# A hybrid recurrent block on one core: weights stored by loaded block, the input stored transposed, and a redone S5 and first feed-forward block

## The chip, the cores and the metric

The kernel runs on one core of a Trainium2 chip. A core has five engines with instruction streams of their own: TensorE (PE; its weight loads are shown apart as PEld), VectorE (DVE), ScalarE (ACT), GpSimd (POOL) and SyncE (SP), which here only issues DMAs. Each stream is executed in its own order; semaphores tie the streams together. Data lie in HBM, in SBUF (128 partitions) and, for the results of TensorE, in PSUM. The metric is the device time of one execution in microseconds (us), the median of the runs.

## The reference, cut to what matters

One trunk layer over 256 latent and 256 context tokens of width 2048, batch 1, all in float32:

```python
mod_x, mod_c = split(silu(c) @ w_mod + b_mod, 6), split(silu(c_ctx) @ w_mod + b_mod, 6)
hx = modulate(rmsnorm(x,   norm_mix), mod_x[0], mod_x[1])      # h * (1 + scale) + shift
hc = modulate(rmsnorm(ctx, norm_mix), mod_c[0], mod_c[1])
cols = h @ w_in                       # 15 column groups, 15376 wide
# four token mixers over cols, forward and backward: HGRN2, retention, S5, mLSTM
# S5: x_t = lam * x_{t-1} + B u_t (complex diagonal, 32 groups of 64 states), y = Re(C x)
y  = sum_j sigmoid(gate_j) * (branch_j @ w_branch[j])
x1 = x + mod_x[2] * (y @ w_out)
h2 = modulate(rmsnorm(x1, norm_mlp), mod_x[3], mod_x[4])
x2 = x1 + mod_x[5] * (square(relu(h2 @ w_ff1)) @ w_ff2)        # 2048 -> 8192 -> 2048
out = rmsnorm(x2, final_norm)
```

All weights together are some 400 MB, read once.

## The kernel before

**Products.** A weight block is loaded as a unit of 256 rows x 512 columns (512 KB, tile `raw`, `unit`, L80) from the row-major weight, so each partition receives two rows of 2 KB. ScalarE rounds it to a high part `wh` (L59), VectorE subtracts to get the low part `wl` (L35), and TensorE adds three products (high x high, low x high, high x low, all at L62) into PSUM. `run_t` gives results with channels on partitions, `run_n` with tokens on partitions; `run_pair` (first feed-forward weight) uses two products, with high and low part of the input side by side. `raw` has four buffers, `wh` and `wl` four each.

**Order.** The program is written as Python generators that are stepped in turn; a scheduler in the framework then places the instructions of each engine by priority. Weight loads and splits run at high priority. What is final is one fixed instruction order per engine; an instruction whose operand is late holds back all behind it on its engine.

**Opening** (`build`, `norm_in`, `mods_in`, `modulate_in`). Parameter rows are loaded by eleven small DMAs and turned into columns by two transposes on TensorE. The tokens are loaded with tokens on partitions, ScalarE sums the squares, VectorE scales each token row. The first two modulations (33.5 MB of `w_mod`) are made in eight rounds of 256 columns: eight loads (`mraw` or `raw`, 128 x 4 x 256, rows of 1 KB), 64 small products into `macc`, a copy, four transposes and three VectorE operations give the columns `modc`. Then two 128-channel pieces of the input are transposed (four transposes each, `m<-ident,x`, L65), modulated by ScalarE from PSUM (`full`), and split into `hh` and `hl`. Beside the rounds run the projections to the S5 input (`gu`, accumulators `g`) and to the mLSTM query (`gq`, accumulators `q`), half a unit at a step. The S5 parameters are loaded after the first round (`s5_load`, L387); `s5_rows` and `s5_cols` work out the powers of the S5 eigenvalues in some 150 small VectorE operations on 32 x 128 tiles, which TensorE then transposes.

**S5.** Time is cut into 128 steps of four tokens. For each of four groups J and two directions d, `s5_weights` builds B and C weights and the table of rotations `E` (complex, 4 x 128) on VectorE, `s5_states` multiplies the inputs `V` by the rotations (`W`), runs a real scan along time (`tensor_tensor_scan`, L609, eight of 128 steps), and rotates back (`X`). TensorE work on the projections to the mLSTM key, value and gate stands between.

**From the output projection to the feed-forward part** (`tail`). For each 512 columns of `w_out` the result is added to the residual `x2`, squares are summed, and the columns are transposed and scaled (`x2T`). When all are there, the reciprocal norm is worked out and broadcast by TensorE (`m<-ident,rs`), VectorE multiplies all of `x2T` by it, and ScalarE and VectorE make the high and low part `h`. Only then does `run_pair` start on `w_ff1`. At the end of a `run_pair` block each of four accumulators is read, added, squared behind the ReLU and split (`ev1`).

## Time and profile before

| | us |
|---|---|
| median of 3 runs | 2060.59 (2057.99 to 2060.61) |
| profiled execution, whole time | 2053.74 |
| profiled execution, span from first to last instruction | 2052.0 |
| TensorE busy | 1964.0 (96%) |
| TensorE weight loads busy | 1611.0 |
| VectorE busy | 1468.0 (72%) |
| ScalarE busy | 1054.5 (51%) |
| DMA | 410.85 MB, mean 200 GB/s |

A busy share is a mean over stages that differ: TensorE is all but full from 700 us on, and has its gaps before that, at the change to the feed-forward part, and at the end. A matmul's own duration (about 390 ns for 512 columns) overlaps with the next; how fast they follow each other is read from the chain or a window, where 156 of them take about 35.5 us.

### The profile page before, as it was taken

What the parts mean: (1) busy time and instruction counts of PE and PEld (TensorE: products, weight loads), DVE (VectorE), ACT (ScalarE), POOL (GpSimd) and SP (SyncE); (2) the same over time, 40 slices, a digit from 0 to 9 for tenths busy, and PEclk for the clock granted to TensorE, in tenths of its full rate; (3) what the DMA queues carried; (4) which work ended last, traced back from release to release, by engine and by line L of the source; (5) the groups of instructions that cost most, each with busy time, mean ns of one, the idle gap of its engine ahead of it and who ended that gap; (6) DMA issues with size and microseconds to landing.
All of it is one profiled execution on the core that took longest, in us unless ns stands there. A gap on an engine that the chain in (4) does not pass through costs nothing.

```text
span 2052.0 us, 30756 instructions
## 1 busy us (share of the span) xinstructions
PE 1964.0 (96%) x11129; PEld 1611.0 (79%) x11129; DVE 1468.0 (72%) x2924; ACT 1054.5 (51%) x1957; POOL 28.2 (1%) x42
## 2 busy tenths in 40 slices
PE   5899999999999999999999999899999999999998
PEld 2566777777988888878888887788888888888886
DVE  2678887587469776888888885677667766666665
ACT  4245445644486555454545455555555445544554
POOL 0000010000000000000000000000000000000000
PEclk9999999999999999999999999999999999999999
DMA  9993212322442456889888876466777676556654
GB/s 325 280 302 102 73 52 83 108 73 68 133 124 83 160 189 201 311 278 315 286 306 296 309 244 236 157 218 224 244 232 225 227 247 187 189 193 192 189 194 154
DMA packets 237652, 410.85 MB, mean 200 GB/s; under 512 B 23064, under 2 KB 58168, under 8 KB 236732
## 3 DMA queue, kind: packets, MB, share of 16 engines
q1 hardware_dynamic: 234864, 402.74, 59.6%
q10 hardware_dynamic: 2636, 6.16, 0.9%
q8 instruction: 87, 1.43, 0.3%
q14 instruction: 65, 0.53, 0.1%
HBM read 406.75 MB, written 2.10 MB: 199 GB/s over the span
## 4 chain that ended last, share of the span: by engine, by line
PE 69%; issue 19%; DVE 5%; DMA 3%; ACT 3%; SPq 1%; POOL 0%; POOLq 0%; DVEq 0%; ACTq 0%
PE g L62 55%; PE m L62 10%; DMA raw<-in_w_mod 2%; DVE wl L35 1%; PE m L65 1%; PE macc L62 1%; ACT wh L59 1%; PE q L62 1%; PE t L62 1%; DVE modacc L53 1%; DVE s5V L609 0%; SPq L387 0%; DMA x<-in_ctx 0%; DVE s5t L35 0%; ACT full L56 0%
## 5 line engine op out<-in xcount | busy, mean ns | idle before, releaser
L59 ACT CAST wh<-raw 128x512 fp32r<-128x512 f32 x1116 | 687.5, 622 | 719.5 <-PE g L62 316.6
L35 DVE TENSOR_TENSOR wl<-raw,wh 128x512 fp32r<-128x512 f32 x1116 | 757.1, 689 | 369.3 <-ACT wh L59 356.2
L62 PE MATMUL g<-wh,hh 128*128 128x512 f32 x832 | 327.6, 394 | 2.4 <-ACT kd L59 2.4
L62 PE MATMUL g<-wl,hh 128*128 128x512 f32 x832 | 327.3, 393 | 0.0
L62 PE MATMUL g<-wh,hl 128*128 128x512 f32 x832 | 326.5, 392 | 0.0
L62 PE MATMUL g<-wh,aT 128*128 128x512 f32 x992 | 307.1, 390 | 0.0
L53 DVE SCALAR_TENSOR_TENSOR modacc<-raw,cx,modacc 128x512 f32<-128x512 f32 x240 | 179.5, 748 | 55.4 <-DMA raw<-in_w_mod 54.4
L62 PEld LDWEIGHTS g<-wh,aT 128*128 128x128 f32 x992 | 186.2, 188 | 39.3 <-ACT wh L59 0.5
L62 PE MATMUL m<-h,wh 128*128 128x512 f32 x512 | 191.9, 398 | 4.5 <-DVE relu L35 4.5
L62 PE MATMUL g<-h,wh 128*128 128x512 f32 x512 | 191.9, 399 | 2.8 <-DVE h L53 2.8
L62 PE MATMUL g<-wl,aT 128*128 128x512 f32 x496 | 193.0, 389 | 0.0
L62 PEld LDWEIGHTS g<-wh,hh 128*128 128x128 f32 x832 | 156.5, 188 | 37.5 <-ACT wh L59 3.4
L62 PEld LDWEIGHTS g<-wh,hl 128*128 128x128 f32 x832 | 156.6, 188 | 32.9 <-issue 1.0
L62 PEld LDWEIGHTS g<-wl,hh 128*128 128x128 f32 x832 | 156.7, 188 | 32.1 <-DVE wl L35 1.1
L62 PE MATMUL g<-hh,wh 128*128 128x512 f32 (+1 forms) x448 | 159.1, 356 | 5.4 <-ACT wh L59 5.4
L62 PE MATMUL g<-hh,wl 128*128 128x512 f32 (+1 forms) x448 | 158.0, 354 | 0.6 <-DVE wl L35 0.5
L62 PE MATMUL g<-hl,wh 128*128 128x512 f32 (+1 forms) x448 | 157.8, 352 | 0.0
L62 PE MATMUL g<-h,wl 128*128 128x256 f32 x512 | 143.6, 281 | 0.0
L62 PE MATMUL m<-h,wl 128*128 128x256 f32 x512 | 143.4, 280 | 0.0
L62 PEld LDWEIGHTS m<-h,wh 128*128 128x128 f32 x512 | 96.6, 189 | 28.7 <-PE m L62 3.4
L62 PEld LDWEIGHTS g<-h,wh 128*128 128x128 f32 x512 | 96.6, 189 | 26.3 <-DVE h L53 3.1
L62 PEld LDWEIGHTS g<-wl,aT 128*128 128x128 f32 x496 | 93.1, 188 | 19.7 <-issue 0.2
(502 smaller groups left out, 2539.0 us busy)
## 6 DMA issues: line engine op xcount, KB each, us to landing
raw<-in_w_ff SPq DMA_DIRECT2D x256, 512.0 KB, 4.0
raw<-in_w_in SPq DMA_DIRECT2D x242, 512.0 KB, 3.8
raw<-in_w_mod SPq DMA_DIRECT2D x160, 512.0 KB, 4.9
mraw<-in_w_mod SPq DMA_DIRECT2D x32, 512.0 KB, 7.4
raw<-in_w_branch SPq DMA_DIRECT2D x32, 512.0 KB, 3.8
raw<-in_w_out SPq DMA_DIRECT2D x32, 512.0 KB, 4.0
x<-in_ctx SPq DMA_DIRECT2D x2, 1024.0 KB
x<-in_x SPq DMA_DIRECT2D x2, 1024.0 KB, 7.1
```

The source lines that it names most:

```text
L35: self.nc.vector.tensor_tensor(out=out, in0=a, in1=b, op=op)
L53: self.nc.vector.scalar_tensor_tensor(out=out, in0=a, scalar=s, in1=b, op0=op0, op1=op1, **kw)
L59: self.nc.scalar.copy(out, a)
L62: self.nc.tensor.matmul(out, lhsT=lhsT, rhs=rhs, start=start, stop=stop, skip_group_check=True, **kw)
L65: self.nc.tensor.transpose(out, in_, self.ident[:n, :n])
```

## The change

The arrays are laid out anew on the host before the launch: each weight as its 256 x 512 blocks in the order of loading, so that a unit is one contiguous 512 KB piece with 4 KB per partition; the tokens transposed to channels x tokens; parameters as columns; the S5 parameters with states on partitions. In the kernel:

- `unit`, `mods_in` and `rest_of_mods` load whole blocks.
- The parameter transposes are gone; `cols1` and `cols2` are two DMAs.
- `norm_in` loads the transposed tokens in four pieces (8 KB per partition), ScalarE squares them, TensorE sums over channels (64 one-column products), the reciprocal norm is broadcast over partitions by TensorE, and VectorE scales all of `x`. `modulate_in` has no transposes.
- `s5_rows` works on 128 x 32 tiles; `s5_c` and the transposes in `s5_cols` are gone.
- The table `E` has 65 instead of 128 rotations (the first half of time turns by the conjugate), with a third, negated plane; a complex turn is three wide operations (`turn`) instead of six; the scans of four state tiles are one scan of 4 x 128 with a zero in the factor at each start (`decay`).
- In `tail` the first block of `w_ff1` starts from the not yet normalised `us`; `normalise` runs beside it, and the block's result is multiplied by the reciprocal norm afterwards (`post1`). The part of the shift, `b1`, comes from a second reading of the first 512 columns of `w_ff1` (4 MB, `shift_cols`) during the output projection.
- `run_pair` reads its accumulators at high priority and does the rest (`post`) behind that.

```diff
     def unit(self, w, row, c0, keep=None):
             raw = self.rawp.tile([128, 2, 512], F32, name="raw")
-            self.nc.sync.dma_start(raw.rearrange("p a (b c) -> p (a b) c", c=n), ap.rearrange("(k p) c -> p k c", p=128))
+            self.nc.sync.dma_start(raw, w[c0 // 512, row // 256])
...
     def run_pair(self, w, c0, x2, evac, post, nk=16, row0=0):
                 if last and k == 1:
-                    evac(j, acc[j][:, :256], acc[j][:, 256:])
+                    with self.tc.high_priority(offset=self.pri):
+                        done.append(evac(j, acc[j][:, :256], acc[j][:, 256:]))
+            if last:
+                for j in range(4):
+                    post(j, done[j])
...
     def norm_in(self, tp, T):
+        x = tp.tile([128, KT, NT], F32, name="x0")
+        ps = self.m()
+        for q in range(4):
+            k4 = slice(4 * q, 4 * q + 4)
+            with self.tc.high_priority(offset=self.pri):
+                nc.sync.dma_start(x[:, k4], i["x_t"][q])
+            sq = T.tile([128, 4, NT], F32, name="sq0", bufs=2)
+            self.act(sq, x[:, k4], AF.Square)
+            for k in range(4):
+                for t in range(4):
+                    self.mm(ps[:, t:t + 1], sq[:, k, 128 * t:128 * t + 128], self.one, start=q == k == t == 0, stop=q == k == 3)
...
+        for k2 in range(8):
+            xk = x[:, 2 * k2:2 * k2 + 2]
+            self.mul(xk, xk, rb[:, None, :].to_broadcast([128, 2, NT]))
...
     def s5_states(self, Pw, P, d, J, sB, E):
-        self.cmul(W[:, 0], W[:, 1], V[:, 0], V[:, 1], E[:, 0], E[:, 1], t, conj=True)
+        self.turn(W[:, :, :, 0:64], t, V[:, :, :, 0:64], rows(slice(63, None, -1)))
+        self.turn(W[:, :, :, 64:], t, V[:, :, :, 64:], rows(slice(1, 65)), conj=True)
+        self.cp(self.decay[:, :, 1:], self.ST[:, 12, dj:dj + 4, None].to_broadcast([128, 4, 127]))
         for q in range(2):
-            for jj in range(4):
-                nc.vector.tensor_tensor_scan(out=V[:, q, jj], data0=self.ST[:, 8, dj:dj + 1].to_broadcast([128, 128]),
-                                             data1=W[:, q, jj], initial=0.0, op0=OP.mult, op1=OP.add)
+            nc.vector.tensor_tensor_scan(out=V[:, q].rearrange("p j a -> p (j a)"), data0=self.decay.rearrange("p j a -> p (j a)"),
+                                         data1=W[:, q].rearrange("p j a -> p (j a)"), initial=0.0, op0=OP.mult, op1=OP.add)
...
     def tail(self, P, PY, yh, yl):
                     self.act(raw[:, kt], ps[:, 256 * k:256 * k + 256], AF.Copy, scale=sc[:, kt:kt + 1])
+                    self.split(us[:, kt, :256], us[:, kt, 256:], raw[:, kt])
...
+                    if early:
+                        self.mul(q, q, rsb)
+                        self.act(q, q, AF.Relu, bias=b1[:, j:j + 1])
+                        self.mul(q, q, q)
...
+                run = self.run_pair(i["w_ff1"], D * g + 512 * cb, us if early else h2, ev1, post1)
+                if early:
+                    for _ in range(2):
+                        next(run)
+                    normalise()
```

How the orders move, at three places. TensorE at the start of the program, before (`pr` are the parameter rows, `macc` the modulation sums, `x_172` and the next three the token tiles):

```order
L65 MATMUL m<-ident,pr_96 128x128
L65 MATMUL m<-ident,pr_103 128x128
L62 MATMUL macc<-mraw,cs 32x256 x16
L62 MATMUL macc<-raw,cs 32x256 x16
L65 MATMUL m<-ident,modsb 128x128 x4
L62 MATMUL macc<-mraw,cs 32x256 x4
L65 MATMUL m<-ident,x_172 128x128
L65 MATMUL m<-ident,x_179 128x128
```

The same place now (`sq` are the squared tokens, `rs` the reciprocal norms that are broadcast):

```order
L62 MATMUL m<-one,sq_128 128x1 x16
L62 MATMUL m<-one,sq_147 128x1 x16
L62 MATMUL m<-one,sq_166 128x1 x16
L62 MATMUL macc<-mraw,cs 32x256
L62 MATMUL m<-one,sq_185 128x1 x16
L62 MATMUL macc<-mraw,cs 32x256 x3
L62 MATMUL m<-ident,rs_203 128x128 x4
L62 MATMUL macc<-mraw,cs 32x256 x12
```

The sums over the tokens stand ahead of nearly all of the first round's modulation products, and no transposes of the input follow the round.

VectorE in one direction of one S5 group, before:

```order
L35 TENSOR_TENSOR s5W<-s5W,s5t 128x512
L35 TENSOR_TENSOR s5t<-s5V,s5E 128x512
L35 TENSOR_TENSOR s5W<-s5W,s5t 128x512
L35 TENSOR_TENSOR wl<-raw,wh 128x512
L609 SCALAR_TENSOR_TENSOR s5V<-s5ST,s5W 128x128 x8
L35 TENSOR_TENSOR s5X<-s5V,s5E 128x256
L35 TENSOR_TENSOR wl<-raw,wh 128x512
L35 TENSOR_TENSOR s5t<-s5V,s5E 128x4x64
```

The same place now (the row at L598 is the scan, as L609 was; `s5dk` is the factor with the zeros):

```order
L35 TENSOR_TENSOR s5t<-s5V,s5E 128x512
L35 TENSOR_TENSOR wl<-raw,wh 128x512
L35 TENSOR_TENSOR s5W<-s5W,s5t 128x8x64
L598 SCALAR_TENSOR_TENSOR s5V<-s5dk,s5W 128x512 x2
L35 TENSOR_TENSOR s5X<-s5V,s5E 128x512
L35 TENSOR_TENSOR wl<-raw,wh 128x512
L35 TENSOR_TENSOR s5t<-s5V,s5E 128x512
```

Eight scans became two, and the rotations back are three operations of 512 instead of six of 256; the number of elements that are rotated is the same.

TensorE from the output projection to the first feed-forward block, before and then now:

```order
L62 MATMUL g<-wl,yh 128x512
L62 MATMUL g<-wh,yl 128x512
L65 MATMUL m<-ident,x_11921 128x128 x8
L62 MATMUL m<-ident,rs_11947 128x128 x2
L62 MATMUL g<-h_12776,wh 128x512
```

```order
L62 MATMUL g<-wl,yhl 128x512
L62 MATMUL g<-wh,yhl 128x512
L62 MATMUL g<-us,wh 128x512
L65 MATMUL m<-ident,x_11716 128x128 x2
L62 MATMUL g<-us,wl 128x256
L62 MATMUL g<-us,wh 128x512
```

The last transposes now stand among products of the new block, and the broadcast of the norm (`m<-ident,rs`) stands 42 rows behind the block's first product instead of ahead of it.

## Rows read from the trace of the kernel before

**Rows 1.** Page, busy time (us, share of span, instructions) and TensorE's busy tenths by slice.
```profile
PE 1964.0 (96%) x11129; PEld 1611.0 (79%) x11129; DVE 1468.0 (72%) x2924; ACT 1054.5 (51%) x1957; POOL 28.2 (1%) x42
...
PE   5899999999999999999999999899999999999998
```

**Rows 2.** Busy us by stage: PE, PEld, DVE, ACT, POOL; clock, DMA share, GB/s.
```profile
0.00:36.00 36.00, 13.17 (x95) 5.39 (x95) 9.06 (x31) 15.38 (x22) 2.65 (x9) 0.91 0.93 319
36.00:173.40 137.40, 122.38 (x1025) 84.13 (x1024) 91.15 (x327) 57.91 (x118) 6.24 (x6) 0.96 0.90 277
173.40:393.50 220.10, 202.25 (x1532) 161.89 (x1530) 176.48 (x400) 119.06 (x274) 10.58 (x12) 0.98 0.25 77
...
700.00:1310.00 610.00, 609.79 (x2847) 503.83 (x2846) 471.73 (x807) 312.79 (x541) 2.16 (x2) 1.00 0.79 267
1310.00:1330.00 20.00, 13.70 (x56) 10.89 (x55) 13.59 (x26) 10.31 (x24) 0.70 (x1) 0.74 0.40 125
```

**Rows 3.** Waits of PE, 0 to 176 us: total us, times, longest.
```profile
PE macc L62 <- DMA raw<-in_w_mod: 8.3, 4, 6.1
PE g L62 <- ACT wh L59: 5.4, 5, 1.4
```

**Rows 4.** Timeline of the opening: start, us, instruction, idle before it.
```profile
35.80 0.50 PE L62 MATMUL g<-hh,wh 128*128 128x512 f32 x1 [0.18 <-ACT wh L59]
...
49.89 4.27 SPq L387 DMA_DIRECT2D s5bt<-in_s_b_re  x1
...
61.83 1.08 PE L62 MATMUL macc<-raw,cs 128*32 128x256 f32 x8 [6.10 <-DMA raw<-in_w_mod]
```

**Rows 5.** DMA rate in 40 slices: 8.75 to 21.25, 24 to 47, 44 to 64 us.
```profile
GB/s 439 349 441 393 419 419 419 419 419 421 444 444 395 419 390 285 203 26 13 10 10 112 0 419 52 52 341 446 419 367 367 472 393 420 419 419 419 419 419 419
...
GB/s 351 351 349 349 349 349 349 345 346 353 347 365 381 374 362 347 347 351 349 349 347 346 351 365 333 338 347 353 345 347 353 347 347 349 362 369 383 356 362 349
...
GB/s 373 383 367 360 352 350 346 352 310 279 247 269 334 312 184 147 99 117 124 8 9 25 100 94 132 145 72 188 279 147 231 270 367 342 334 350 363 375 377 369
```

**Rows 6.** Chain of waits in the opening: start, us, what.
```profile
64.08 5.49 PE g L62 x12
...
86.65 2.95 PE g L62 x12
89.60 0.44 PE m L65 x4
...
108.47 1.00 PE macc L62 x16
109.47 1.63 PE q L62 x12
```

**Rows 7.** VectorE by shape, 40 to 400 us: busy us, mean ns, idle before.
```profile
L609 DVE TENSOR_TENSOR_SCAN s5V<-s5ST,s5W 128x128 f32<-128x128 f32 x64 | 21.5, 402 | 0.0
L35 DVE TENSOR_TENSOR s5E<-s5E,s5t 128x512 f32<-128x512 f32 x16 | 11.0, 689 | 0.3
...
L35 DVE TENSOR_TENSOR s5X<-s5X,s5t 128x256 f32<-128x256 f32 x16 | 6.7, 419 | 0.1
...
L774 DVE TENSOR_TENSOR_SCAN de<-one,dlf 64x256 f32<-64x256 f32 x2 | 1.3, 669 | 0.0
```

**Rows 8.** Busy us in two S5 groups, columns as in rows 2.
```profile
208.00:254.50 46.50, 42.82 (x346) 35.57 (x345) 40.71 (x92) 23.09 (x56) 4.28 (x6) 1.00 0.23 72
254.50:302.70 48.20, 43.34 (x346) 35.47 (x345) 40.89 (x93) 23.64 (x58) 4.18 (x4) 1.00 0.19 60
```

**Rows 9.** Timeline of TensorE at the change to the feed-forward part.
```profile
1317.65 0.88 PE L65 MATMUL m<-ident,x 128*128 128x128 f32 x6 [1.96 <-DVE x L35]
...
1319.88 1.22 PE L62 MATMUL m<-ident,rs 128*128 128x128 f32 x4 [1.36 <-POOL rs L246]
...
1323.90 0.79 PE L62 MATMUL g<-h,wh 128*128 128x512 f32 x1 [2.79 <-DVE h L53]
```

**Rows 10.** Waits of PE, 1330 us to the end: total us, times, longest.
```profile
PE m L62 <- DVE relu L35: 4.5, 6, 1.2
```

More of the change, by code (lines that the diff above doesn't have):

```diff
@@ L74, in cmul, with turn @@
         self.tt(pi, pi, t, OP.subtract if conj else OP.add)
+    def turn(self, out, t, x, rows, conj=False):
+        sh = list(out.shape)
+        bc = lambda v: v[:, None].to_broadcast(sh)
+        self.mul(out, bc(x[:, 0]), rows(1, 0) if conj else rows(1, 2))
+        self.mul(t, bc(x[:, 1]), rows(2, 1) if conj else rows(0, 1))
+        self.add(out, out, t)
     def split(self, h, l, src):
@@ L96, in unit @@
                 self.split(h, l, raw[:, k])
-                for q in range(512 // n):
-                    H.append(h[:, n * q:n * q + n])
-                    L.append(l[:, n * q:n * q + n])
+                H.append(h)
+                L.append(l)
         return H, L
@@ L512, in s5_cols @@
+        for T, first in ((lo, None), (hi[:, 1:3], b)):
+            if first is None:
+                nc.vector.memset(T[:, 0, :, 0:1], 1.0)
+                nc.vector.memset(T[:, 1, :, 0:1], 0.0)
+            else:
+                nc.vector.tensor_copy(T[:, :, :, 0], b)
             n = 1
-            while n < cnt:
+            while n < 8:
                 bb = [b[:, q_, :, None].to_broadcast([128, 32, n]) for q_ in range(2)]
@@ L1186, in b_k @@
         for u in range(8):
-            h, l = self.unit(self.w_in[256 * u:256 * u + 256, 3072:3584])
+            h, l = self.unit(self.w_in, 256 * u, 3072)
             last = u == 7
@@ L1265, in last_block, with shift_cols, tail @@
         evac(1, acc[1])
-    def tail(self, P, yh, yl):
+    def shift_cols(self, P, ring, out, sh):
+        acc = P.tile([128, 512], F32, name="modacc", bufs=1)
+        for u in range(8):
+            with self.tc.high_priority(offset=self.pri):
+                raw = ring[:, u % 4]
+                self.nc.sync.dma_start(raw, self.i["w_ff1"][0, u])
+                for k in range(2):
+                    c = sh[:, 2 * u + k:2 * u + k + 1]
+                    if u == k == 0:
+                        self.ts(acc, raw[:, k], c, OP.mult)
+                    else:
+                        self.stt(acc, raw[:, k], c, acc, OP.mult, OP.add)
+            yield
+        ps = self.tps.tile([128, 512], F32, name="t")
+        for a in range(4):
+            self.mm(ps[:, a:a + 1], acc[:, 128 * a:128 * a + 128], self.one, start=True)
+        self.cp(out, ps[:, :4])
+    def tail(self, P, PY, yh, yl):
         nc, i = self.nc, self.i
@@ L1273, in tail @@
         self.tickp = None
-        while 3 not in self.modcol:
-            next(self.ticks)
+        for _ in self.ticks:
+            pass
         mrow = P.tile([128, D], F32, name="mrow", bufs=2)
@@ L1557 @@
     arrays, ins = {}, {}
[L1558 to L1559 removed]
+    for name, a in _layout({n: np.asarray(a) for n, a in inputs.items()}).items():
         arrays[f"in_{name}"] = a
```

351 lines of the change are left out of this document (168 added, 183 removed).

## The prediction

> **What bounds the kernel now.** I read the busy time and the slices first: TensorE is busy for 96% of the span, and only its first slices stand clearly below nine tenths [rows 1]. The stage table then says where the missing 4% lie. From 700 to 1310 us TensorE is busy for 609.8 of 610 us: nothing that leaves its work as it is can shorten this stage. The places with room are the stretch to 36 us (13.2 busy), the rest of the opening from 36 to 173.4 us (122.4 of 137.4), the S5 stage to 393.5 us (202.3 of 220.1), and 1310 to 1330 us (13.7 of 20, at a mean granted clock of 0.74) [rows 2]. Which engine ends the waits there comes from the lists of waits, the timeline and the chain.
>
> In the opening it is the DMA. Its share is 0.90 to 0.93 to 173 us [rows 2]; TensorE's largest wait is for the modulation weights, 8.3 us, 6.1 of it at once at 61.8 us [rows 3, 4]. The rate shows why. While rows of 1 KB are loaded the engines are full and move about 349 GB/s (second line); the 8 KB rows of the tokens move 419 (first line); and from 51 to 57 us, where the S5 parameters come in pieces of 64 bytes, the rate falls to between 8 and 184 (third line) [rows 5]. One such load holds SP's queue for 4.27 us [rows 4], and every weight load stands behind it.
>
> In the S5 stage two engines are nearly full: in a group of 46.5 us VectorE is busy for 40.7 and TensorE for 42.8 [rows 8]. At the change to the feed-forward part TensorE waits 1.96 us for the residual, 1.36 for the norm, 2.79 for the first normalised piece [rows 9].
>
> **The change part by part.**
>
> *Opening.* Its loads are 64 of 512 KB for the modulations, 16 of 512 KB for two projections, 4 of 1 MB for the tokens and about 1 MB for S5: 47 MB. At 349 GB/s that is 135 us; with rows of 4 KB or more I take 400, between the 349 of 1 KB and the 419 of 8 KB [rows 5], and get 118 us. With a start at 2.5 us the last load would land at 121 us (115 to 138 at the two ends). So TensorE becomes the limit. Its work from the first projection product on, at rows' durations: 192 products of `g` at 2.95/12 = 0.246 us, 47.2; 192 of `q` at 1.63/12, 26.1; seven rounds of 64 `macc` at 1.00 per 16, 28.0; their transposes 7 x 0.44, 3.1; 16 S5 transposes, 1.8 [rows 6]: 106 us. The 14 x 4 input transposes (14 x 0.44 = 6.2 us) and some 3 us of S5 transposes are gone.
>
> When does the first projection product start? Before at 35.8 us [rows 4]. Now the tokens land by about 13 us (4.2 MB at 419), the squares and 64 one-column products follow, then the broadcast, then eight VectorE products of 1024 elements. 256 and 512 elements take 0.42 and 0.69 us [rows 7], so 1024 take about 1.22, eight 9.8. These stand on VectorE ahead of the first modulation columns. The one-column products are not in the rows; between 0.05 us (they stay hidden behind the loads) and 0.25 us each (16 us in all), the start comes out between 27 us, when the first round's loads are through (8.4 MB, 23.5, and 3 us of columns), and 42 us. I take 36, no gain. Then the opening ends at 36 + 106 = 142 us if nothing stalls, against 173.4. For stalls I add 4 us: each round has to pass copy, transposes, VectorE and ScalarE once, and the S5 parameter operations (about 150 of some 0.2 us) sit between weight splits in VectorE's queue. VectorE was busy for 91 of 137 us here [rows 2], so it has cover for 5 us more of scaling, but not for a late split in front of TensorE. **Opening: 27 us saved**; the ends are 8 (only the hole of the S5 loads goes) and 35 (start at 31, no stall).
>
> *S5 stage.* Per direction and group, by elements [rows 7]: the table `E` was six operations of 512 (4.1 us) and is four of 224 and one of 448 (about 0.39 and 0.62, 2.2 us): 1.9 saved. The turn back was six of 256 (2.5) and is three of 512 (2.1): 0.4. The additions in B and C, two into one twice: 0.3. The turn into `W` has the same elements in the same six operations: nothing. The scans: 64 took 21.5 us, 0.336 each, 2.7 per direction; a scan's price per element from 128 (402 ns) to 256 steps (669) is 2.1 ns, so one of 512 takes 1.2, two 2.4: 0.3. Together 2.9, and 5.8 of the 40.7 us per group. ScalarE gets four small copies and one factor copy of 508 elements per direction, about 1.5 us beside 23 of 46.5 busy [rows 8]; the factor copy lies beside the turn. If VectorE set the pace, a group would fall from 47 to 41 us; but TensorE is busy for 42.8 of the group [rows 8], part of that the overlapping ends of products, so it takes over at about there. I take 4 us per group, and four groups less the weights that are made in the opening: **15 us saved**. Ends: 0 (the chain through ScalarE and TensorE sets the pace) and 25.
>
> *Change to the feed-forward part.* The block starts on `us` while the norm is worked out. The three waits, 6.1 us, go. The clock is at 0.74 here [rows 2], that is for about half of the 20 us at the lower of its two levels, and at that level twelve products took 5.49 instead of 2.95 us [rows 6]: some 2.5 us on the 5 us of work that TensorE had there. What is late next: VectorE, with eight splits of a unit (11 us), eight products of 512 and sixteen subtractions of 256 (12 us), in a block that lasts TensorE 22 us (64 products of 512 and 64 of 256 columns). I leave 1 us for it. The 16 additional splits and 16 multiply-adds in the output projection lie under TensorE, whose stage to 1310 us has VectorE at 472 of 610 us [rows 2]; if that cover were gone, they would cost up to their own 19 us (16 at 0.42, 16 at about 0.75). The 4 MB more of DMA lie there too. **8 us saved**, 2 to 9.
>
> *Early reading of accumulators.* TensorE waits 4.5 us for `relu` in six places [rows 10]; **3 us saved**, 0 to 4.
>
> *Weight layout later.* From 700 us on the DMA had spare time (0.79, 267 GB/s) and TensorE none [rows 2]: nothing.
>
> The sum is 27 + 15 + 8 + 3 = 53 us. On the profiled execution (span 2052.0 and 1.7 around it, 2053.7) that gives 2000.7; the median of the runs lies 6.9 above that execution, and 2060.6 - 53 = 2007.6. Small unpriced gains (eleven parameter loads less, S5 tables) I put at 3: **2004 us**.
>
> The Trainium skill (DMA: Bandwidth & Descriptors, section "Where 436 GB/s comes from") speaks against the layout: transfers from HBM are bound at about 358 GB/s per core, whatever the rows. By it the 349 seen with 1 KB rows could not grow, the loads would land at 134 us, and the opening would end some 4 us later than above. The trace doesn't agree: 419 GB/s hold over many slices [rows 5], though for 4 MB only.
>
> **The rivals.**
>
> 1. *The layout brings no rate.* The loads run on at 349 GB/s and land at 138 us; the last units need some 10 us more, so the opening ends near 149 instead of 146, and the time is 2007. For it: no row here shows 4 KB rows at length; against it: the 8 KB rows. The Trainium skill's bound named above is this case. Chance 0.08.
>
> 2. *The opening keeps its pace.* The loads are faster, but buffers and the in-order queues make TensorE wait round by round: after the hole, TensorE still needed 109 us from 64 to 173, and of the round's loads only four `raw` buffers serve both projections and modulations. Only the hole goes, 8 us, and the S5 stage gains a third, 5: 2060.6 - 8 - 5 - 11 = 2037. For it: the 5.4 us of waits for ScalarE's split [rows 3]; against it: the DMA share of 0.9 says that the loads, not the buffers, were the pace. Chance 0.2.
>
> 3. *More.* Both stages reach their ends: 35 + 25 + 9 + 4 = 73 us, 1988. For it: VectorE's 40.7 us in a group sit in one dependent chain; against it: TensorE's own work in a group. Chance 0.17.
>
> 4. *Slower.* Contiguous blocks are read at a worse rate, all partitions of a block from one stretch of memory. The stage from 700 to 1310 us moves 163 MB; to lose the 53 us it would have to take 663 us, so this decides below 163/663 = 246 GB/s. At 230 GB/s the stage takes 709 us and the time is 2004 + 99 = 2103. For it: no row shows such blocks; against it: 419 GB/s with the tokens, which were contiguous too. Chance 0.05.
>
> **How the numbers follow.** The forecast has 0.5, with a range of its own of 1992 to 2020. About 0.2% (4 us) is what a measurement of this kernel can tell from no change. Faster: 0.5 + 0.08 + 0.2 + 0.17 = 0.95, less 0.02 for a second rival in which the other gains fail too; same 0.02; slower 0.05. The range reaches from between the forecast and the third rival's end to just past the second rival: 1978 to 2040.
>
> **What would show it.** Right: a DMA rate of 390 or more in long stretches of the opening; no slices of 8 to 184 GB/s where the S5 parameters load; the last `q` product at 140 to 152 us; about 43 us per S5 group, VectorE at 35 of it; no wait over 1 us between the output projection and `us`, and a clock of 1.00 there; the `relu` waits below 2 us. Wrong: the last `q` product after 160 us with the DMA idle in between (second rival), the rate at 350 (first), a stage after 700 us with TensorE waiting for weights (fourth), or an S5 group that still takes 46 us with VectorE at 35, which would say that another chain than VectorE's set its pace.

## The result: 0.55% slower, and where the time went

The changed kernel takes 2071.0 us (median of 5 runs, 2066.2 to 2071.8) against 2060.6 for the kernel before: ratio 1.0055, 95% interval 1.0044 to 1.0065. Its profiled execution has a span of 2069.2 us, 17.2 more than that of before; the medians differ by 10.4, as the profiled execution of before is itself 6.9 us faster than its median. Forecast was 2004.

The page of the changed kernel, busy time and tenths by slice, to be held against [rows 1]:

```profile
PE 1991.4 (96%) x11098; PEld 1635.4 (79%) x11098; DVE 1455.0 (70%) x2848; ACT 1070.9 (52%) x2002; POOL 26.9 (1%) x40
...
PE   7798999999999999999999999999999999999998
...
DMA  5784211422343375888898878567777776666664
```

TensorE is busy for 27 us more, although transposes were taken away. The stages of the changed kernel, columns as in [rows 2] (the number behind POOL's is the mean granted clock: 1.00 is TensorE's higher level, 2.4 GHz, 0.50 the lower, 1.2 GHz). The first three answer to the first three rows there, cut at the same instructions:

```profile
0.00:58.30 58.30, 37.69 (x220) 32.49 (x220) 12.68 (x30) 16.22 (x19) 4.61 (x10) 0.96 0.57 218
58.30:187.60 129.30, 117.17 (x860) 77.71 (x860) 77.86 (x310) 57.09 (x119) 3.02 (x3) 0.94 0.77 285
187.60:408.60 221.00, 203.71 (x1531) 164.82 (x1530) 158.83 (x307) 127.60 (x300) 10.57 (x12) 0.96 0.25 77
715.20:1236.10 520.90, 520.79 (x2434) 430.29 (x2432) 417.96 (x726) 262.66 (x448) 1.64 (x1) 1.00 0.81 275
1236.10:1341.70 105.60, 101.19 (x446) 80.22 (x446) 71.06 (x115) 55.59 (x110) 0.53 (x1) 0.97 0.70 235
1341.70:1361.70 20.00, 19.98 (x118) 17.21 (x118) 17.82 (x36) 15.56 (x36) 0.70 (x1) 1.00 0.59 178
```

The last three rows are the stage up to the output projection, the output projection, and the 20 us behind it. In the kernel before, the output projection and the gap behind it are:

```profile
1217.50:1314.90 97.40, 97.34 (x445) 78.58 (x444) 57.99 (x89) 52.96 (x98) 0.53 (x1) 1.00 0.63 214
1314.90:1323.90 9.00, 2.70 (x14) 1.78 (x13) 6.43 (x14) 5.58 (x16) 0.70 (x1) 0.71 0.56 173
```

The start is 22.5 us longer and the DMA engines idle in it (share 0.57 instead of 0.93); the rest of the opening is 8 shorter; the S5 stage is as long as before, though VectorE is busy for 18 us less in it; the output projection (1236 to 1342) is 8 longer and has TensorE idle; the 20 us behind it are full, where 6 were idle. The same milestones in all kernels that matter below, read from their traces (us from the span's start; e1 to e13 are the experiments; "its last product" is given some 0.2 us before its end, where a next product can follow):

| | before | changed | e1 | e2 | e11 | e13 |
|---|---|---|---|---|---|---|
| first projection product | 35.8 | 58.3 | 36.0 | 31.8 | 30.9 | 31.2 |
| last query product | 173.6 | 187.8 | 167.5 | 168.9 | 161.5 | 162.1 |
| S5 output product | 367.1 | 382.2 | 363.8 | 362.4 | 355.5 | 352.9 |
| output projection starts | 1217.5 | 1236.1 | 1217.2 | 1215.1 | 1207.9 | 1206.3 |
| its last product | 1314.9 | 1341.7 | 1319.9 | 1312.6 | 1311.7 | 1306.7 |
| feed-forward part starts | 1323.9 | 1341.7 | 1319.9 | 1321.6 | 1311.7 | 1306.8 |
| first product on `aT` | 1419.7 | 1435.0 | 1411.8 | 1417.5 | 1403.8 | 1399.6 |
| last product on `h` | 1955.1 | 1972.8 | 1948.9 | 1954.1 | 1940.0 | 1937.0 |

From milestone to milestone the changed kernel is 22.5 us slower, 8.3 faster, 0.9 slower, 3.5 slower, 8.2 slower, 9.0 faster, 2.5 faster and 2.4 slower than the kernel before; the end brings 0.5 back. That makes the 17.2.

TensorE in the first 60 us of the changed kernel, in order of time:

```profile
12.55 20.64 PE L62 MATMUL m<-one,sq 128*128 128x1 f32 x96 [12.55 <-ACT sq L56]
33.12 1.06 PE L62 MATMUL macc<-mraw,cs 128*32 128x256 f32 x2
34.11 6.99 PE L62 MATMUL m<-one,sq 128*128 128x1 f32 x32
41.03 1.07 PE L62 MATMUL macc<-mraw,cs 128*32 128x256 f32 x6
...
44.66 2.75 PE L62 MATMUL macc<-mraw,cs 128*32 128x256 f32 x24
47.23 1.91 PE L62 MATMUL macc<-raw,cs 128*32 128x256 f32 x32
...
58.31 0.79 PE L62 MATMUL g<-hh,wh 128*128 128x512 f32 x1 [6.80 <-ACT wh L59]
```

The 64 one-column products are 128 records (two passes each) and fill TensorE from 12.6 to 41.1 us. Nearly all of the first round's modulation products stand behind them, and these hold the buffers. The DMA queue's own waits to 60 us, and the engines in the middle of that stretch (columns as in rows 2):

```profile
SPq L333 <- PE macc L62: 30.5, 2, 27.3
```

```profile
23.75:42.00 18.25, 18.25 (x85) 16.62 (x84) 0.33 (x2) 1.91 (x1) 0.41 (x1) 1.00 0.00 1
```

A load waited 27.3 us for a buffer, and for 18 us nothing was loaded (share 0.00). Here a busy TensorE is the bottleneck and not the sign of a good stage.

The clock of 1.00 in this row is not a measurement: the trace has no record of the clock before 47.2 us, and the column counts such time as full. The products show the level. Just before 47.2 us 24 products of `macc` take 2.75 us, just behind it 32 of the same shape take 1.91, at twice the pace. So TensorE ran at the lower of its two levels until then, through all of the one-column products. (The clock in the first row of the stages, 0.96 here and 0.91 in [rows 2], is too high for the same reason.)

### The profile page after: what moved, and what is told of

Read it like the earlier page. It is cut to its first block, busy times and chain, and to the rows that moved or that the text cites. A ratio compares the mean times of both kernels' runs of the same rounds, so it can differ in the third digit from the quotient of the medians.

```text
span 2069.2 us, 30584 instructions
## 1 busy us (share of the span) xinstructions
PE 1991.4 (96%) x11098; PEld 1635.4 (79%) x11098; DVE 1455.0 (70%) x2848; ACT 1070.9 (52%) x2002; POOL 26.9 (1%) x40
## 5 line engine op out<-in xcount | busy, mean ns | idle before, releaser
L62 PEld LDWEIGHTS g<-wh,hh 128*128 128x128 f32 x832 | 156.9, 189 | 35.8 <-ACT wh L59 3.4
L62 PE MATMUL m<-h,wh 128*128 128x512 f32 x480 | 180.2, 399 | 1.8 <-DVE relu L35 1.8
L62 PE MATMUL g<-h,wh 128*128 128x512 f32 x480 | 180.3, 400 | 0.0
L62 PE MATMUL m<-h,wl 128*128 128x256 f32 x480 | 134.7, 281 | 0.0
L62 PE MATMUL g<-h,wl 128*128 128x256 f32 x480 | 134.7, 281 | 0.0
L62 PEld LDWEIGHTS m<-h,wh 128*128 128x128 f32 x480 | 90.2, 188 | 25.3 <-DVE relu L35 3.0
L62 PEld LDWEIGHTS g<-hh,wh 128*128 128x128 f32 x448 | 86.2, 193 | 28.2 <-ACT wh L59 10.6
```

The costliest lines, as they stand in the source:

```text
L62: self.nc.tensor.matmul(out, lhsT=lhsT, rhs=rhs, start=start, stop=stop, skip_group_check=True, **kw)
```

## The experiments

Ratios are to the kernel before, run beside it on the same chip, with 95% intervals; the changed kernel has 1.0055. Milestones and waits are those of one profiled execution of each kernel.

| run | median us | ratio |
|---|---|---|
| e1 wide sums | 2043.4 | 0.9929 (0.9916 to 0.9943) |
| e2 blocks only | 2055.0 | 0.9988 (0.9978 to 0.9997) |
| e3 old boundary | 2067.2 | 1.0036 (1.0023 to 1.0048) |
| e4 second reading in the ring | 2069.2 | 1.0055 (1.0043 to 1.0068) |
| e5 e1, reading from the second block | 2048.1 | 0.9948 (0.9932 to 0.9965) |
| e7 e1, old S5 operations | 2047.0 | 0.9944 (0.9930 to 0.9957) |
| e8 e1, old boundary | 2039.8 | 0.9914 (0.9898 to 0.9929) |
| e9 e1, three buffers | 2048.3 | 0.9962 (0.9947 to 0.9978) |
| e10 e1, reading from the third block | 2042.1 | 0.9915 (0.9901 to 0.9928) |
| e11 e1, folded scale | 2038.8 | 0.9900 (0.9887 to 0.9914) |
| e12 e11, old boundary | 2038.5 | 0.9899 (0.9885 to 0.9914) |
| e13 e11 and e10 | 2036.3 | 0.9891 (0.9876 to 0.9905) |
| e14 e13 without S5 parameters | 2032.5 | 0.9873 (0.9854 to 0.9893) |
| e15 e1, two buffers | 2052.3 | 0.9962 (0.9949 to 0.9976) |
| e16 e1 again, beside e15 | 2044.9 | 0.9928 (0.9915 to 0.9941) |

**e1, the sums.**

```diff
-            sq = T.tile([128, 4, NT], F32, name="sq0", bufs=2)
+            sq = T.tile([128, 4, NT], F32R, name="sq0", bufs=2)
...
-                for t in range(4):
-                    self.mm(ps[:, t:t + 1], sq[:, k, 128 * t:128 * t + 128], self.one, ...)
+                self.mm(ps, ones, sq[:, k], start=q == k == 0, stop=q == k == 3)
```

(then a copy and four transposes turn the sums into columns.)

> Edit: the changed kernel, with the column sums of the squared tokens made by 16 products of 512 columns against a constant matrix of ones instead of 64 products of one column against 64 different squared tiles. Theory A (the one-column products, 27.6 us of TensorE from 12.6 to 41.1 us, hold up the first round's modulation products and with them the loads): the 16 products take about 4 us (16 x 0.23), the sums are there at about 15 us, the first projection product starts at 31 to 37 us instead of 58.3, and most of these 22 to 27 us reach the end: 2044 to 2052 us against 2071. Rival B (the opening is paced by the loads and rounds anyway): the first projection product comes earlier, but the last query product stays within 8 us of 187.6, and the time is 2063 to 2071.

TensorE at the start of e1:

```profile
11.17 3.83 PE L62 MATMUL m<-sq,ones 128*128 128x512 f32 x8 [11.17 <-ACT sq L56]
15.30 1.19 PE L62 MATMUL m<-sq,ones 128*128 128x512 f32 x4 [0.29 <-ACT sq L56]
...
17.11 1.21 PE L62 MATMUL m<-sq,ones 128*128 128x512 f32 x4
...
35.98 1.22 PE L62 MATMUL g<-hh,wh 128*128 128x512 f32 x2 [6.08 <-ACT hh L59]
```

The sums take 6.2 us of TensorE instead of 27.6, the first projection product comes at 36.0, and 1.0055 - 0.9929 = 0.0126, 26 us, are back. Theory A holds: this one form of a sum cost the change its sign. Two things came with the edit, and e1 does not part them: there are fewer passes, and TensorE reached its higher level earlier. The first eight of the wide products take 3.83 us, the next four 1.19, and the trace's first record of the clock, at the higher level, is at 14.8 us, between the two. In the changed kernel the rise came at 47.2 us, behind the one-column products.

**e2, the layout alone.** `unit`, `mods_in` and `rest_of_mods` of the changed kernel in the kernel before, all else as before.

> Edit: the kernel before, with only the weights stored by loaded blocks; tokens, parameters, S5 and the change to the feed-forward part as before. Theory A (the layout raises the rate of the opening's loads from about 349 to about 400 GB/s and does no harm later): the 47 MB of the opening take some 15 us less, part of which the rounds give back; the last query product at 162 to 168 us instead of 173.4 and 2049 to 2056 us against 2060.6. Rival B (TensorE and the buffers pace the opening): last query product within 4 us of 173.4, 2057 to 2061. Rival C (the blocks are read worse, or disturb the products: some stages of the changed kernel have 0.232 instead of 0.227 us per product): 2064 or more.

The rate of e2 from 24 to 47 us, where [rows 5] has 349 in the second line:

```profile
GB/s 420 406 392 435 399 413 406 399 435 392 420 406 399 428 392 413 413 385 420 392 406 427 385 435 378 435 413 385 427 385 427 413 399 356 286 311 313 385 170 154
DMA packets 5531, 8.89 MB, mean 386 GB/s; under 512 B 3435, under 2 KB 3465, under 8 KB 5530
```

The rate rises as forecast (a mean of 386 with some small parameter loads in it), and the time falls by only 0.12%. The last query product comes 4.7 us earlier, of which the earlier start makes 4.0; from the first projection product to it the opening takes 137.1 us, as before (137.8). Between A and B, by the ratio nearer to B: once loads are faster, something else sets the pace.

**e3, the old boundary.** The changed kernel with the `tail` of before (early reading of the accumulators kept).

> Edit: the changed kernel with the change to the feed-forward part as before (no block on the not yet normalised input, no second reading of 4 MB of the first feed-forward weight); the early reading of the accumulators stays. Theory A (the new way saves 9 us of waits and 2.5 us of a slow first block, but its 4 MB in the first quarter of the output projection stop VectorE and cost 8 us there): the output projection takes 98 instead of 106 us, the waits of 6 us come back, and the time is 2070 to 2077 against 2071. Rival B (the new way is worth all of its gain, and the output projection is longer for another reason, such as the new weight layout): output projection still about 105 us, time 2079 or more. Rival C (the new way costs more than it brings): 2066 or less.

The output projection, the boundary and the later feed-forward blocks of e3:

```profile
1235.60:1333.10 97.50, 97.45 (x445) 78.49 (x444) 57.83 (x89) 52.89 (x98) 0.53 (x1) 1.00 0.67 215
1333.10:1341.60 8.50, 2.23 (x14) 1.35 (x12) 6.45 (x14) 5.60 (x15) 0.70 (x1) 0.84 0.58 185
1434.50:1967.50 533.00, 532.61 (x2697) 451.19 (x2696) 357.47 (x613) 272.69 (x489) 0.00 (x0) 1.00 0.68 213
```

The feed-forward part starts at 1341.6 with the old boundary and at 1341.7 with the new: the 8.5 us saved at the boundary are paid in the output projection (105.6 instead of 97.5 us). That part of A holds; the ratio is 0.0019 lower, 4 us, with intervals that just overlap, between A and C; in the profiled executions the later blocks take 533.0 instead of 537.8 us (below).

**e4, e5, e10, the second reading.** What stops the output projection? VectorE of the changed kernel in it, and TensorE's two waits:

```profile
1249.30 0.75 DVE L53 SCALAR_TENSOR_TENSOR modacc<-fa,modcol,modacc 128x512 f32<-128x512 f32 x1 [3.02 <-DMA fa<-in_w_ff]
1249.97 1.29 DVE L35 TENSOR_TENSOR wl<-raw,wh 128x512 fp32r<-128x512 f32 x2
...
1250.71 0.50 PE L62 MATMUL g<-wl,yhl 128*128 128x512 f32 x1 [2.07 <-DVE wl L35]
...
1264.97 4.51 PE L62 MATMUL m<-bmr,ident 128*128 128x512 f32 x6 [2.34 <-DVE bmr L35]
```

At the first, VectorE stands at a multiply-add whose load has not landed; the weight split behind it waits, and TensorE for that. The second (`bmr`, the bias row of the modulation) does not stand behind such a multiply-add: VectorE was idle for 1.28 us before it, and the profile names nothing that it waited for. The waits are 4.4 of the 8.2 us. Behind each the clock fell to the lower level; the three rows below lack 1.7, 1.1 and 0.6 us of full clock, 3.4 in all:

```profile
1248.00:1258.00 10.00, 7.93 (x28) 5.99 (x27) 7.92 (x13) 2.56 (x5) 0.00 (x0) 0.83 1.04 405
1258.00:1268.00 10.00, 7.66 (x26) 4.97 (x25) 6.02 (x10) 3.04 (x6) 0.00 (x0) 0.89 0.96 348
1268.00:1278.00 10.00, 10.00 (x39) 7.03 (x39) 7.45 (x12) 5.33 (x10) 0.00 (x0) 0.94 0.76 285
```

e4, e5 and e10 put the loads into the weight buffers' own ring, e5 and e10 also start them later:

```diff
-                raw = ring[:, u % 4]
+                raw = self.rawp.tile([128, 2, 512], F32, name="raw")
...
+            if cb == 1:      # e10: cb == 2
+                self.ticks, self.tick_rate = self.shift_cols(P, ring, b1, sh), 0.4      # e10: 0.6
```

> Edit: the changed kernel, where the second reading of 4 MB takes its turn in the ring of the weight buffers, one unit after every three or four of the output projection, instead of a ring of its own that is filled at once in the first quarter. Theory A (VectorE's wait for these early loads holds up the weight splits): the output projection falls from 105.6 to 97 to 100 us, and the time to 2063 to 2066. Rival B (4 MB and 12 us of VectorE more cost the same wherever they lie): output projection 104 to 106, time 2069 to 2073.

e4 came out as rival B: 105.8 us for the output projection, no gain. But a wait of the same kind is there in another place, VectorE and TensorE of e4:

```profile
1264.58 1.54 DVE L53 SCALAR_TENSOR_TENSOR modacc<-raw,modcol,modacc 128x512 f32<-128x512 f32 x2 [5.68 <-DMA raw<-in_w_ff]
1266.04 0.68 DVE L35 TENSOR_TENSOR tmp<-g,mrow 128x512 f32<-128x512 f32 x1
...
1267.55 0.66 PE L65 MATMUL m<-ident,x 128*128 128x128 f32 x2 [3.54 <-issue]
```

VectorE waits 5.68 us for a load, with the multiplication of the residual (`tmp`) behind it. TensorE's wait of 3.54 us ends, by the order of time, with the residual that comes of it; the profile names no releaser.

> Edit: the kernel of the wide sums, where the second reading of 4 MB takes its turn in the ring of the weight buffers and begins only with the second of the four blocks of the output projection. Theory A (in the first 20 us of the output projection the residual, the final norm's row and the weights already fill the DMA engines, 0.85 to 0.98 of their time, so the extra units land late there and VectorE waits for them in front of what TensorE needs; later there is room at a share of 0.6): output projection 97 to 99 us instead of 102.7, 2036 to 2040 us against 2043.4. Rival B (4 MB and 12 us of VectorE more cost the same wherever they lie): 102 to 104 us, 2042 to 2045.

A was missed, and B too: 108 us. The loads run at high priority, so the first two were issued 15 and 22 us after the start of the output projection, where the DMA engines are full (share 0.96 and then 0.88); VectorE waited 6.1 us for one. e10 begins late enough:

> Edit: the kernel of the wide sums, where the second reading of 4 MB takes its turn in the ring of the weight buffers and begins only with the third of the four blocks of the output projection; in the run that began with the second block its first two units were still issued in the first 20 us, and VectorE waited 6.1 us for one of them with the residual's multiplication behind it. Theory A (the stop comes from these units in the crowded first 20 us alone): no wait of VectorE over 1 us for these loads before the second block, output projection 97 to 100 us instead of 102.7 to 108, ratio to the kernel before 0.990 to 0.992 (2037 to 2041 us where that takes 2058). Rival B (any unit that VectorE has to fetch in its order stops the weight splits behind it, wherever it lies): the waits move to the second half, output projection 102 to 108, ratio 0.993 to 0.996.

```profile
1213.70:1313.10 99.40, 97.60 (x446) 78.44 (x446) 70.56 (x115) 55.27 (x110) 0.53 (x1) 1.00 0.76 250
```

99.4 us, and no wait of VectorE over 1.3 us for these loads. A holds for the stage: the same 4 MB and the same VectorE work cost 2 us here and 8 there. (Where the loads stay in the first quarter the stage scatters, from 102.7 us in e1 to 105.6 in the changed kernel and 108.7 in e15.) Of the whole time the ratio is 0.0014 lower than e1's, 3 us, with overlapping intervals.

**e7, the S5 operations.** e1 with the S5 tables, weights, turns and scans of before.

> Edit: the kernel of the wide sums with the S5 operations of before on the new parameter layout (table of 128 rotations, complex products in six operations, eight scans instead of two). Theory A (VectorE does not set the pace of the S5 stage; TensorE's own work and a few waits at fixed places do): VectorE some 15 us more, the stage from the last query product to the S5 output product still 193 to 198 us (196.3 with the new operations, 193.5 in the kernel before), and 2041 to 2046 us against 2043.4. Rival B (the new operations bring what was forecast, 15 us, and only the extra copies on ScalarE or another loss hide it): the stage is 206 us or longer, 2053 or more.

The S5 stage of e7, then of e1:

```profile
165.90:362.20 196.30, 177.82 (x1395) 142.35 (x1395) 160.68 (x367) 101.23 (x246) 10.59 (x12) 0.97 0.23 69
```

```profile
167.50:363.80 196.30, 178.49 (x1394) 144.97 (x1395) 143.21 (x272) 110.06 (x271) 10.58 (x12) 0.95 0.23 71
```

VectorE is busy for 17.5 us less and the stage is as long to the tenth: A (its time, 2047.0, lies 1 us above A's range). The groups did get shorter: from one group's first scan to the next e7 takes 48.4, 49.1 and 46.7 us, e1 40.7, 44.8 and 45.2. What they gave went into the stretch from the last group's first scan to the S5 output product, e7 and then e1:

```profile
327.20:362.20 35.00, 33.52 (x162) 26.76 (x161) 25.20 (x56) 21.32 (x47) 0.00 (x0) 1.00 0.38 110
```

```profile
315.60:363.80 48.20, 46.45 (x220) 37.80 (x219) 28.42 (x42) 25.23 (x53) 0.00 (x0) 1.00 0.39 120
```

TensorE has the same products to do in the stage; where the groups are shorter, 58 more of them are left for its end. Over the kernels with the new operations it scatters from 190.8 (e13) to 198.8 us (e12), with the old from 193.5 to 196.3.

**e8 and e12, the old boundary on the better opening.** Edits as e3, on e1 and on e11.

> Edit: the kernel of the wide sums with the change to the feed-forward part as before (no block on the not yet normalised input, no second reading). Theory A (as in the run with the old boundary and the old sums, where this brought 4 us: 8 us of the output projection against 8.5 us of waits and 2.5 of a slow first block, and 4 to 5 us because the normalised input lies at another place in memory and its products follow at 0.232 instead of 0.236 us): output projection 97.5 us, the feed-forward products at 0.232, 2037 to 2041 us against 2043.4. Rival B (the 4 us were chance): 2043 to 2048.

> Edit: the kernel of the folded scale with the change to the feed-forward part as before. Theory A (both gains add up: 2 to 5 us at the start, 3 us from the boundary): ratio to the kernel before 0.987 to 0.990, 2032 to 2038 us where that takes 2058. Rival B (the folded scale brings nothing): 0.991 to 0.992, as in the run with the wide sums and the old boundary.

e8 lies at 0.9914 against 0.9929: the direction of A, within the intervals. e12 equals e11 (0.9899 and 0.9900): its ratio is at the edge of A's range, but the two gains do not add up, as A says. As long as the second reading stops VectorE, the two boundaries are worth about the same.

**e9 and e15, buffers.** `mraw` with 3, then with 2 instead of 4 buffers; e16 repeats e1 beside e15.

> Edit: the kernel of the wide sums with three instead of four buffers for the first half of each round's modulation weights. Theory A (after the first projection product the opening is paced by the return of buffers through TensorE's in-order queue: the loads waited 34.5 us for the sums of the modulations to free them): the last query product 8 to 15 us later than 167.5, 2050 to 2058 us. Rival B (something else paces it: TensorE's own work at the lower clock, or VectorE's small S5 operations between the weight splits): within 3 us, 2041 to 2047.

> Edit: the kernel of the wide sums with two instead of four buffers for the first half of each round's modulation weights (three had 0.9962, and in its profile no loss). Theory A (the return of buffers paces the opening): the last query product at 175 us or later (167.5 with four, 166.4 with three), 10 to 25 us more than the wide sums on the same chip. Rival B (TensorE's work, its clock and the waits of each round's chain pace it, and four buffers have slack): last query product within 4 us of 167.5, within 5 us of the wide sums beside it; then the 0.3% of three buffers was chip and scatter.

> No edit to the kernel of the wide sums: it runs beside the one with two buffers, for a comparison on one chip. Expected: 0.991 to 0.994 of the kernel before, last query product 165 to 169 us.

The last query product comes at 166.4 us with three buffers, at 167.5 (e1) and 165.8 (e16) with four, and at 174.7 with two. TensorE's waits for these loads to 190 us, of e15:

```profile
PE macc L62 <- DMA mraw<-in_w_mod_a: 10.4, 11, 2.1
```

In e1 they are 2.0 us. So two buffers begin to bite, just short of what A asked for, and by the milestones four have slack: the return of buffers is not what paces the opening with the wide sums. The times say it less clearly. With three, the ratio is 0.3% above e1's, beyond both intervals and between A and B; the runs scatter from 2043 to 2060, and the profiled one lost nothing. Where the others lost it stays open.

**e11, the scale.** (In the runs with the folded scale the tile `decay` is also allocated later, at its first use.)

```diff
-        for k2 in range(8):
-            xk = x[:, 2 * k2:2 * k2 + 2]
-            self.mul(xk, xk, rb[:, None, :].to_broadcast([128, 2, NT]))
...
+            self.stt(x[:, kt, t], x[:, kt, t], col[:, 1, 1 - s, kt:kt + 1], self.rb[:, t], OP.mult, OP.mult)
```

> Edit: the kernel of the wide sums, where the input is not scaled by the reciprocal norm in eight operations ahead of the first modulation columns, but by VectorE together with the modulation, two operations of 256 elements per 128 channels, each after its columns. Theory A (the 9.2 us of scaling stand in front of the columns on VectorE and put off the first projection product, which is the start of the chain): first projection product at 29 to 32 us instead of 36.0, last query product 2 to 5 us before 165 to 167.5, ratio to the kernel before 0.990 to 0.992 (0.993 with the scaling ahead). Rival B (from the first product on the loads and the clock set the pace, so an earlier start is given back): last query product at 165 to 168, ratio 0.993 or more.

VectorE in e1 and then in e11:

```profile
23.03 9.17 DVE L35 TENSOR_TENSOR x<-x,rb 128x1024 f32<-128x1024 f32 x8 [2.97 <-ACT rb L59]
32.12 0.25 DVE L351 TENSOR_REDUCE modc<-m 128x4 f32<-128x16 f32 x2
```

```profile
26.81 0.26 DVE L349 TENSOR_REDUCE modc<-m 128x4 f32<-128x16 f32 x2 [6.44 <-PE m L65]
...
27.57 1.67 DVE L53 SCALAR_TENSOR_TENSOR x<-x,modc,rb 128x256 f32<-128x256 f32 x4
```

The columns come 5.3 us earlier, the first projection product at 30.9, the last query product at 161.5, and the ratio falls to 0.9900: A.

**e13 and e14.** e13 joins e11 and e10; e14 tests what still holds the opening.

> Edit: the folded scale and the second reading that begins with the third block, together, on the kernel of the wide sums. If the two gains add up (5 us at the start, 4 us in the output projection): 2031 to 2036 us where the kernel before takes 2058, ratio 0.987 to 0.989. If a gain at the start is given back before the output projection, or the early block still costs something: 0.990 or more.

> Edit: the kernel of e13, where the S5 parameters are not worked out: the table of the eigenvalues' powers is filled with 0.5 in six operations instead of some 100 small ones (about 18 us of VectorE between 55 and 105 us); the rest runs on these numbers. Theory A (these operations stand ahead of weight splits on VectorE, and TensorE waits for the splits, some 6 us in three places between 59 and 94 us, with a lower clock behind each): the last query product 6 to 12 us before that of e13, ratio lower by 0.003 to 0.006. Rival B (TensorE's waits there have another cause, or are taken over by the next: loads, ScalarE's casts, the round's own chain): within 3 us of e13, ratio lower by less than 0.0015.

e13 is the fastest complete version, 2036.3 us, 0.9891 (0.9876 to 0.9905), 22 us below the kernel before. It lies just outside the range for gains that add up, and its interval overlaps with those of e11 and e12. e14's last query product comes 4.6 us before e13's, between A and B, and its end only 0.7 us earlier in the profiled executions; the two ratios' intervals overlap. So by one execution each VectorE's small S5 operations are a part of the opening's pace, not the main one.

## Why the prediction was wrong, point by point

*Start.* The step that failed is the price of the one-column products, from 0.05 us each, hidden behind the loads, to "0.25 us each (16 us in all)", and with it a start between 27 and 42 us ("I take 36, no gain"). Each took 27.6/64 = 0.43 us, none of it hidden: TensorE's order shown in the section on the change has them ahead of the products that free the buffers. In the sum's own terms 27 + 27.6 makes 55 us; it was 58.3. The chain behind the sums made the start: they end at 41.1 us, the scaling that needs them at 54.6, and the first projection product follows:

```profile
45.39 9.18 DVE L35 TENSOR_TENSOR x<-x,rb 128x1024 f32<-128x1024 f32 x8 [3.89 <-ACT rb L59]
```

The loads were stopped too, but that cost nothing that shows: the rest of the opening is no longer than in e1 (129.5 and 131.5 us). With the sums made otherwise the start came at 36.0. That this is the number I took is in part luck, as it was a choice between two ends; the scaling ahead of the columns, 9.8 us in my sum, measured 9.17.

Why 0.43? The price is that of the weight loads at the lower clock. The loads of the squared tiles (PEld) are busy for 27.5 of the 27.6 us. Equal loads of the transposes show what the level does, `rs` before the rise at 47.2 us and `modsb` behind it:

```profile
L62 PEld LDWEIGHTS m<-one,sq 128*128 128x128 f32 x128 | 27.5, 332 | 13.4 <-ACT sq L56 12.5 <-issue 0.8
...
L62 PEld LDWEIGHTS m<-ident,rs 128*128 128x128 f32 x8 | 1.8, 327 | 1.4 <-POOL rs L238 1.4
...
L65 PEld LDWEIGHTS m<-ident,modsb 128*128 128x128 f32 x4 | 0.4, 140 | 1.2 <-ACT modsb L59 1.2
```

And products of the very same form, one column with a fresh 128 x 128 float32 tile, stand in the trace of the kernel before, where the clock was 1.00:

```profile
1218.53 0.95 PE L62 MATMUL t<-one,modacc 128*128 128x1 f32 x8
```

By their starts, its eight passes follow each other every 0.111 us, those of the changed kernel's sums every 0.213. I had said that these products are not in the rows, but they are in that trace: two passes are 0.22 us, within my range. By an estimate from it the 128 passes take 14 us at the higher level. What I left out is that TensorE can be at the lower level there, and stay at it.

The Trainium skill (TensorE: Matmul & The Clock Gate, section "LDWEIGHTS (loading the stationary operand)") says that such a load's time goes by its columns, about 107 ns for 128. By that estimate the 128 loads are 14 us. The trace agrees at the higher level (0.111 us), and not at the lower one, where each takes twice that (0.213).

*The rest of the opening.* Forecast 106 us of work and 4 of stalls; it took 129.3 (before 137.8), and 131 in e1 and e13. Faster loads do not shorten it (e2), nor do four buffers pace it (e9, e15). Where the 21 us beyond my 110 come from, two stretches of e1 show:

```profile
36.00:60.00 24.00, 20.42 (x149) 12.23 (x150) 8.81 (x41) 7.45 (x14) 0.00 (x0) 0.87 0.73 266
60.00:90.00 30.00, 24.08 (x153) 15.55 (x152) 27.08 (x152) 7.92 (x15) 0.00 (x0) 0.83 0.80 295
```

For some 30% of these 54 us the clock was at the lower of its two levels, which costs about 8 us; and TensorE is idle for 15 us between the first projection product and the last query product. With the 106 us of work that makes 129 of e1's 131.5. I had priced stalls at 4 and the clock at none. The second rival had TensorE wait round by round, with 0.2, for buffers and in the queues' order (e9 and e15 speak against the buffers); the S5 operations are some 4 us of it (e14), the rest stays open.

*S5 stage.* VectorE's work fell from 40.7 to about 33.5 us per group, and the groups got shorter, as forecast ("about 43 us per S5 group"): from one group's first scan to the next 45.9, 47.6 and 47.6 us before, 41.6, 41.7 and 45.5 in the changed kernel. The step that failed is to count four such savings as the stage's: 15 us forecast, none measured. The stretch from the last group's first scan to the S5 output product, before and then in the changed kernel:

```profile
331.60:367.10 35.50, 33.76 (x162) 26.54 (x161) 25.35 (x56) 21.40 (x46) 0.00 (x0) 1.00 0.36 110
```

```profile
334.00:382.20 48.20, 46.42 (x221) 37.77 (x219) 28.39 (x42) 25.23 (x53) 0.00 (x0) 1.00 0.39 120
```

The projection products that had stood between the groups now stand behind the last one (162 records of TensorE there before, 221 now), and the stage ends when TensorE is through with them. My own row said it, with TensorE busy for 42.8 of 46.5 us; I let TensorE set the pace of a group and not of the stage. What else is left are waits of TensorE: 17.8 us before, 17.3 in the changed kernel, 17.8 in e1. A faster VectorE did not remove them; those for its own `s5X` even rose, from 4.4 to 6.6 us.

*Change to the feed-forward part.* The three waits and the low clock went as forecast (-9.0 and -2.5 us). Failed: "The 4 MB more of DMA lie there too", under TensorE at no price. The rows had only the mean DMA share of 700 to 1310 us, 0.79, and not the first 20 us of the output projection (from 1248 to 1258 us the engines are full), and I had not asked what stands behind the new instructions on VectorE while they wait. Price 8.2 us, of it 4.4 of waits and 3.4 of lower clock behind them; e10 gives back 6.

*Early reading.* Right: the waits for `relu` fell from 4.5 [rows 10] to 1.8 us, in e3 to none, and the later feed-forward blocks from 535.4 (before) and 536.6 (e2, old reading) to 533.0 us (e3). In the changed kernel itself they take 537.8, as its products on `h` are slower (last section).

*Later layout.* No wait for weights came or went, as said: 520.79 of 520.90 us busy. But the branch products and the feed-forward products run a little slower, some 3 and 4 us. e2, which has the layout alone, keeps the branch products at their old pace, so for these it is not the layout.

*Rivals.* The first (no rate) and the fourth (blocks read worse) are out by e2's 386 GB/s; with it the 358 GB/s that the Trainium skill states (DMA: Bandwidth & Descriptors, "Where 436 GB/s comes from") are exceeded over 8.9 MB, with one core at work. None of my rivals had the slowdown that came: a part that I had priced and not doubted.

## What to carry to other kernels

When a sum over partitions is moved to TensorE, make the data the moving operand and a constant the stationary one. Price an instruction that the rows do not show by its nearest relative in the trace, pass by pass, and at the lower clock too where TensorE has not yet been at the higher one; where the clock has no record, read the level from the pace of equal instructions. Before an added instruction is costed at nothing, ask what stands behind it in its engine's order while its operand is late, and read the cover from the 20 us where it will stand, not from the stage's mean. A saving in each group is not one of the stage, as long as another engine has the same work to finish in it.

## What the runs showed of the hardware

- A product of one column with a fresh 128 x 128 float32 operand has two passes. At the higher level they follow each other every 0.111 us (`t<-one,modacc`, 0.22 us a product), at the lower every 0.213 us (`m<-one,sq`, 0.43). The same sums with a constant operand of ones, the squares rounded to float32r and 512 columns moving: 16 products in 6.2 us, half of them at the lower level, and no load of a fresh operand.
- In the changed kernel TensorE was busy from 12.6 to 41.1 us, nearly all with one-column products, and at the lower level throughout; in e1 the ninth of the 16 wide products was at the higher.
- Blocks of 4 KB per partition load at a mean of 386 GB/s (some small loads among them), rows of 1 KB at 349, the tokens' 8 KB rows at 419.
- Equal products of 512 columns follow each other at different distances, by operand. Median distance of their starts: 0.227 us for `hh` in every kernel; for `brh` 0.227 in the kernel before and e2, 0.232 in the changed kernel and all built on it; for `h` 0.232 or 0.233 with the old boundary, and where `h` lies in the place of `y` 0.235 or 0.236, but 0.233 in e5. So the place of the tile alone does not say it. I did not test it, and the cause stays open.
